# One shared probability tile for both key blocks in a sliding-window attention, and square roots on ScalarE for the last norms

## The chip, the cores and the metric

The kernel runs on one core of a Trainium2 chip. The core has a matrix engine (PE, with its weight loads shown as PEld), a vector engine (DVE), a scalar engine (ACT), a general engine (POOL), and a queue engine (SP) that issues most transfers. Each engine works through its own instructions in a fixed order; semaphores order them between engines. POOL and ACT issue some transfers too; a transfer that adds to what its target holds is issued by POOL.

The metric is the device time of one execution in microseconds, the median of several runs. Before the change it is 973.95 us (three runs, 972.76 to 975.39).

## The reference

The reference is one layer of a hybrid decoder: 1024 rows and 16 meta rows ahead of them, 1024 columns, in float32.

```python
u = rmsnorm(h, g_pre_mix)
q, k, v, xr, yr = split(u @ w_in)          # 512, 128, 128, 512, 512 columns
attn = sliding_window_attention_with_sinks(q, k, v, sinks)   # 8 heads of 64, 2 key heads, window 128
xr = causal_depthwise_conv(xr, conv_w, conv_b)
rec = gelu(yr) * rg_lru(xr, ...)           # gates, then a scan over the rows
h = h + rmsnorm(concat(attn, rec) @ w_out, g_post_mix)
u = rmsnorm(h, g_pre_ffn)
h = h + rmsnorm(square(relu(u @ w_ff1)) @ w_ff2, g_post_ffn)
return h[:, 16:]
```

In attention, rows are padded in front to a multiple of 128. A block of 128 query rows sees the block of keys before it and its own block. With `diff` the query's position less the key's, a key is valid where 0 <= diff < 128. So in the previous block, query row p sees the key columns c > p, and in its own block the columns c <= p: each of the 128 column numbers is valid in exactly one of the two blocks. For the first block of queries the previous block holds only the 16 meta rows; its other columns are invalid. A sink per head enters the maximum and the denominator of the softmax.

## The kernel before

**Precision.** A float32 product is made of reduced-precision ones (fp32r): each operand is split into a high part (a cast on ACT) and a low remainder (a subtraction on DVE; `split`, lines 93 to 100), and `mm3` (lines 121 to 125) adds three matmuls: high by high, high by low, low by high. These three lines are the largest groups of the profile, whatever the stage.

**Stages.** Rows are normed, transposed and projected in four pieces (lines 230 to 352). `fills` (line 570) holds ten more projections, queries, recurrent inputs and gates. Attention (lines 432 to 523) goes over four head pairs `j`, and for each over two halves of four query blocks: `scores(j, half, q)`, then the next projection by `next_fill`, marked as less urgent by 1000 places (`deferred`), then `attend` for the pair-half before. Then come the gates and the scan of the recurrence (`gates`, `decay`, `recur`, `rec_out`), the output projection, its norm, and the two feed-forward products, made by a Strassen-like plan of sums of quarter matrices. The last product has seven plan entries `i` with eight steps `q` each (`steps`, line 1082); the last three steps of the last entry are run row tile by row tile, each followed by `finish_late`.

**What sets the order.** Within a stage the instructions are written in program order, and the framework orders each engine's instructions ahead of time by priority and by when its own simulation has them ready; `behind` pins single instructions behind others, and `lut` pins the order of table functions on ACT. On the chip the order of each engine is fixed. Buffers come from pools by tag; `bufs` (line 55) gives their number: 8 of tag c, 17 of tag b, 2 of tag raw, 2 of tag e, and so on. An instruction that needs a buffer waits until the last user of it is done.

**Scores.** For each of two heads of the pair-half, and two blocks at a time, PE writes scores against both key blocks, 256 columns, to PSUM (lines 447 and 451). One fused DVE instruction adds the mask, takes the minimum with the negated sink, and writes the negated masked scores with their minimum (`tensor_tensor_reduce`, line 467; `mask1` for block 0). ACT takes the exponential of 257 columns (256 and the sink) with its sum (`lut`, line 474). DVE scales by the reciprocal (line 480).

**Values.** `attend` transposes the 256 probability columns of each of four blocks as two 128x128 tiles (line 495), splits them into high and low, and multiplies with the values. Two neighbouring query blocks share a key block, so a key block's values are the stationary operand for 256 columns, except at the ends (128): ten matmuls a head (line 506, in `av`). Halves of the result are added (lines 520 and 521).

**The values themselves** are transposed from `vt` and split by `put_v` (lines 409 to 422); `vm` holds the 16 meta rows, zero below, and `km` their keys.

**The last stage.** `fetch_2` loads the weights of a step; where a sum of two quarters is wanted, either both are loaded and added on DVE, or the second is added by an accumulating POOL transfer (line 1055). `LASTW` (line 1041) names the buffers for the steps of the last entry: (tag, None) means one buffer with an accumulating transfer. `finish_early` norms the row tiles 4 to 7 and adds them to the output in DRAM by an accumulating transfer. `finish_half` prepares the second half of the tiles 0 to 3, `finish_late` ends them: the tiles 0 and 1 as the early ones, the tiles 2 and 3 with rows read back (`h`) and added by DVE, and two plain stores each. The inverse root of a norm is taken by POOL, as a power of -0.5 (`rstd_of`, line 164, and line 1173).

Of the kernel before, what the change touches and what calls it, by code (L numbers as in the profile page):

```python
# [37 lines left out]
def hybrid_layer(  # L38
# [128 lines left out]

    def load_cols(cols, tag="ws"):
        raw = slot("raw", [P, KC, P])
        o = 0  # L170
        for c0, n in cols:
            w, lo = c0
            nc.sync.dma_start(
                raw[:, :, o : o + n],
                w[:, lo : lo + n].rearrange("(k p) c -> p k c", p=P),
            )
            o += n
        hi, lo_ = pair(tag, [P, KC, P])
        split(hi, lo_, raw)
        return hi, lo_  # L180
# [45 lines left out]
    nc.vector.tensor_copy(vm.rearrange("p a b -> p (a b)"), zero[:, :256])  # L226
# [80 lines left out]
    def sink_k(acc, t0, n):  # L307
        o = 0
        if t0 == 0:
            m = slice(0, NMETA)  # L310
            put_k(
                [km[:, 0, m], km[:, 1, m]], [km[:, 2, m], km[:, 3, m]], acc[:, m]
            )
            o = NMETA
# [8 lines left out]
    def new_q():  # L323
# [3 lines left out]
        def sink_q(acc, t0, n):  # L327
            c = slice(t0 - NMETA, t0 - NMETA + n)
            for h in range(2):
                r, o = HALF[h], HALF[1 - h]  # L330
                split_scaled(q[h][r, c], q[h][o, c], acc[r], HD ** -0.5)
# [25 lines left out]
    for c in range(NLRU):  # L357
# [7 lines left out]
    mask = const.tile([P, 256], F32, name="mask")  # L365
    nc.gpsimd.memset(mask, 0.0)
    nc.gpsimd.affine_select(
        out=mask[:, 0:P], in_=mask[:, 0:P], pattern=[[1, P]], compare_op=ALU.is_gt,
        fill=NEG, base=0, channel_multiplier=-1,
    )  # L370
    nc.gpsimd.affine_select(
        out=mask[:, P:256], in_=mask[:, P:256], pattern=[[-1, P]],
        compare_op=ALU.is_ge, fill=NEG, base=0, channel_multiplier=1,
    )
    mask1 = const.tile([P, 256], F32, name="mask1")
    nc.gpsimd.memset(mask1[:, 0:P], NEG)
    nc.gpsimd.memset(mask1[:, 0:NMETA], 0.0)
    nc.gpsimd.affine_select(
        out=mask1[:, 0:NMETA], in_=mask1[:, 0:NMETA], pattern=[[1, NMETA]],
        compare_op=ALU.is_gt, fill=NEG, base=P - NMETA, channel_multiplier=-1,  # L380
    )
    nc.gpsimd.tensor_copy(mask1[:, P:256], mask[:, P:256])
# [30 lines left out]

    pv = bank("o")
    nc.tensor.transpose(pv[:NMETA, :P], vt[:, :NMETA], ident)
    put_v([vm[:NMETA, 0, :], vm[:NMETA, 1, :]], pv[:NMETA, :P])
    for b in range(2):
# [4 lines left out]
        put_v([vk[0][:, 4 * b : 4 * b + 4, :], vk[1][:, 4 * b : 4 * b + 4, :]], pv)  # L422
# [9 lines left out]
    def scores(j, half, q):  # L432
        sn = [slot("c", [P, 4, 257]) for _ in range(2)]
# [3 lines left out]
        for h in range(2):  # L437
            nc.vector.tensor_copy(
                sn[h][:, :, 256], nsink[:, j + 4 * h : j + 4 * h + 1].to_broadcast([P, 4])
            )  # L440
        for bp in range(2):
            for h in range(2):
# [21 lines left out]
                for i in range(2):  # L464
                    b = 4 * half + 2 * bp + i
                    k = 2 * bp + i
                    nc.vector.tensor_tensor_reduce(
                        out=sn[h][:, k, 0:256], in0=sp_[:, i, :],
                        in1=mask1 if b == 0 else mask, scale=-1.0,
                        scalar=nsink[:, j + 4 * h : j + 4 * h + 1],  # L470
                        op0=ALU.add, op1=ALU.min, accum_out=negm[:, h, k : k + 1],
                    )
                    lut(
                        sn[h][:, k, :], sn[h][:, k, :], AF.Exp, scale=-1.0,
                        bias=negm[:, h, k : k + 1], accum_out=den[:, h, k : k + 1],
                    )
        for h in range(2):
            nc.vector.reciprocal(rden[:, h, :], den[:, h, :])
            for k in range(4):
                nc.vector.tensor_scalar(  # L480
                    sn[h][:, k, 0:256], sn[h][:, k, 0:256], rden[:, h, k : k + 1],
                    None, op0=ALU.mult,
                )
        return sn

    def attend(j, half, sn):
        flat = [t_.rearrange("p a b -> p (a b)") for t_ in sn]
        for h in range(2):
            ph, pl = pair("c", [P, 1024])
            for bp in range(2):  # L490
                pt = bank("pt")
                for i in range(2):
                    for s in range(2):
                        o = (2 * i + s) * P
                        nc.tensor.transpose(  # L495
                            pt[:, o : o + P],
                            sn[h][:, 2 * bp + i, s * P : (s + 1) * P], ident,
                        )
                c = slice(512 * bp, 512 * bp + 512)
                split(ph[:, c], pl[:, c], pt)  # L500
            po = bank("o")

            def av(kb, oc, n, pc, first, last):
                v = vm[:, h, :] if kb == 0 else vk[h][:, kb - 1, :]
                for k, p_ in enumerate((ph, pl)):
                    nc.tensor.matmul(  # L506
                        po[:, oc : oc + n], v, p_[:, pc : pc + n],
                        start=first and k == 0, stop=last and k == 1,
                        skip_group_check=True,
                    )  # L510

            kb0 = 4 * half
            av(kb0, 0, P, 0, True, False)
            for i in range(3):
# [767 lines left out]
```

## Time and profile before

| what | value |
|---|---|
| median of three runs | 973.95 us |
| the profiled execution, in all | 972.95 us |
| its span | 971.1 us |
| granted clock of PE | 0.999 |
| busy: PE, DVE, ACT, POOL | 953.7, 674.6, 502.0, 82.4 us |
| transposes of probabilities (line 495) | 128, 128x128 |
| value matmuls (line 506) | 96 of 256 columns, 64 of 128 columns |
| first and last start of the value matmuls | 73.9 and 216.8 us |
| fused mask and minimum (line 467) | 64, 0.48 us each |
| last matmul of PE starts | 963.7 us |

Times in the views are microseconds from the span's start, and ns where marked. PE's matmuls are pipelined: one's busy time overlaps the next one's, so the cost of a matmul in a row is read from start to start, not from its busy time. In a timeline, a line gives start, length, engine, line of the kernel, operation, what is written and read, and in square brackets the engine's idle time before it with what ended it. The chain is the run of work that ended last, followed back from the end.

### The profile page before, as it was taken

What the parts mean: (1) busy time and instruction counts of PE and PEld (TensorE: products, weight loads), DVE (VectorE), ACT (ScalarE), POOL (GpSimd) and SP (SyncE); (2) the same over time, 40 slices, a digit from 0 to 9 for tenths busy, and PEclk for the clock granted to TensorE, in tenths of its full rate; (3) what the DMA queues carried; (4) which work ended last, traced back from release to release, by engine and by line L of the source; (5) the groups of instructions that cost most, each with busy time, mean ns of one, the idle gap of its engine ahead of it and who ended that gap; (6) DMA issues with size and microseconds to landing.
All of it is one profiled execution on the core that took longest, in us unless ns stands there. A gap on an engine that the chain in (4) does not pass through costs nothing.

```text
span 971.1 us, 12490 instructions
## 1 busy us (share of the span) xinstructions
PE 953.7 (98%) x4782; PEld 803.0 (83%) x4782; DVE 674.6 (69%) x997; ACT 502.0 (52%) x809; POOL 82.4 (8%) x109
## 2 busy tenths in 40 slices
PE   6999999999999999999999999999999999999997
PEld 6999999888878887888888878888888888888786
DVE  6679997775976686665645465468557676779694
ACT  6646673567844554343555556555433344445350
POOL 4100000000002100000000000000111000003152
PEclk9999999999999999999999999999999999999999
DMA  9002001012234466576522264323678765548923
GB/s 296 23 1 66 23 23 44 23 48 64 84 119 144 159 207 209 173 251 209 198 87 87 97 206 125 114 87 114 172 176 198 186 224 187 184 163 195 223 80 87
DMA packets 88219, 130.13 MB, mean 134 GB/s; under 512 B 13624, under 2 KB 52552, under 8 KB 88160
## 3 DMA queue, kind: packets, MB, share of 16 engines
q1 hardware_dynamic: 79792, 107.33, 33.4%
q0 software_dynamic: 7792, 20.45, 10.1%
q10 hardware_dynamic: 576, 1.57, 0.4%
q8 instruction: 37, 0.61, 0.2%
q14 instruction: 22, 0.18, 0.1%
HBM read 110.46 MB, written 18.87 MB: 133 GB/s over the span
## 4 chain that ended last, share of the span: by engine, by line
PE 89%; DVE 4%; DMA 3%; issue 2%; ACT 1%; POOL 0%; SPq 0%; POOLq 0%; DVEq 0%; ACTq 0%
PE ps_acc L124 11%; PE ps_acc L123 11%; PE ps_acc L125 11%; PE ps_s L125 6%; PE ps_pt L123 6%; PE ps_s L124 6%; PE ps_pt L125 6%; PE ps_s L123 6%; PE ps_pt L124 6%; PE ps_o L124 5%; PE ps_o L123 5%; PE ps_o L125 5%; PE ps_o L506 2%; PE ps_pt L495 1%; DMA raw<-in_w_ff_dram 1%
## 5 line engine op out<-in xcount | busy, mean ns | idle before, releaser
L95 ACT CAST ws<-raw 128x1024 fp32r<-128x1024 f32 (+1 forms) x69 | 70.7, 1024 | 126.6 <-PE ps_o L124 48.8
L98 DVE TENSOR_TENSOR ws<-raw,ws 128x1024 fp32r<-128x1024 f32 (+1 forms) x70 | 83.5, 1194 | 59.6 <-ACT ws L95 59.5
L123 PE MATMUL ps_acc<-a,ws 128*128 128x256 f32 (+2 forms) x272 | 90.5, 333 | 0.6 <-DVE b L305 0.6
L124 PE MATMUL ps_acc<-a,ws 128*128 128x256 f32 (+2 forms) x272 | 89.8, 330 | 0.0
L125 PE MATMUL ps_acc<-a,ws 128*128 128x256 f32 (+2 forms) x272 | 89.4, 329 | 0.0
L98 DVE TENSOR_TENSOR b<-b,b 128x1024 fp32r<-128x1024 f32 (+2 forms) x48 | 57.6, 1201 | 24.7 <-PE ps_o L124 17.1
L95 ACT CAST ws<-e 128x1024 fp32r<-128x1024 f32 x43 | 45.0, 1046 | 55.3 <-PE ps_o L124 28.1
L95 ACT CAST b<-b 128x1024 fp32r<-128x1024 f32 (+2 forms) x48 | 49.4, 1030 | 42.8 <-DVE b L788 40.0
L98 DVE TENSOR_TENSOR ws<-e,ws 128x1024 fp32r<-128x1024 f32 x43 | 52.6, 1222 | 21.6 <-ACT ws L95 21.6
L123 PEld LDWEIGHTS ps_acc<-a,ws 128*128 128x128 f32 x272 | 51.2, 188 | 4.9 <-DVE b L305 0.8
L125 PEld LDWEIGHTS ps_acc<-a,ws 128*128 128x128 f32 x272 | 51.2, 188 | 4.6
L124 PEld LDWEIGHTS ps_acc<-a,ws 128*128 128x128 f32 x272 | 51.2, 188 | 3.9
L164 POOL TENSOR_TENSOR rs<-ms,half_pow 128x1 f32<-128x1 f32 (+1 forms) x31 | 21.3, 692 | 356.5 <-DVE ms L160 355.1
L123 PE MATMUL ps_acc<-ws,b 128*128 128x512 f32 (+1 forms) x120 | 46.3, 386 | 0.4 <-ACT ws L95 0.4
L124 PE MATMUL ps_acc<-ws,b 128*128 128x512 f32 (+1 forms) x120 | 46.5, 388 | 0.2 <-DVE ws L98 0.2
L125 PE MATMUL ps_acc<-ws,b 128*128 128x512 f32 (+1 forms) x120 | 46.2, 385 | 0.0
L123 PE MATMUL ps_pt<-ws,b 128*128 128x512 f32 x112 | 44.1, 394 | 0.0
L124 PE MATMUL ps_pt<-ws,b 128*128 128x512 f32 x112 | 44.1, 394 | 0.0
L125 PE MATMUL ps_pt<-ws,b 128*128 128x512 f32 x112 | 44.0, 393 | 0.0
L123 PE MATMUL ps_s<-ws,b 128*128 128x512 f32 x110 | 43.4, 395 | 0.0
L124 PE MATMUL ps_s<-ws,b 128*128 128x512 f32 x110 | 43.3, 393 | 0.0
L125 PE MATMUL ps_s<-ws,b 128*128 128x512 f32 x110 | 43.3, 393 | 0.0
(381 smaller groups left out, 2690.1 us busy)
## 6 DMA issues: line engine op xcount, KB each, us to landing
raw<-in_w_ff_dram SPq DMA_DIRECT2D x62, 512.0 KB, 4.0
e<-in_w_ff_dram SPq DMA_DIRECT2D x45, 512.0 KB, 3.6
d<-in_w_ff_dram SPq DMA_DIRECT2D x12, 512.0 KB, 3.8
s_dram<-d POOLq DMA_DIRECT2D x12, 512.0 KB, 3.9
raw<-in_w_in_dram SPq DMA_DIRECT2D x9, 512.0 KB, 3.6
c<-in_x_dram SPq DMA_DIRECT2D x8, 512.0 KB, 8.5
d<-in_x_dram SPq DMA_DIRECT2D x8, 512.0 KB, 4.6
out_dram<-raw SPq DMA_DIRECT2D x8, 512.0 KB, 2.6
```

The costliest lines, as they stand in the source:

```text
L95: nc.scalar.copy(hi, src)
L98: low = nc.vector.tensor_tensor(lo, src, f32(hi), op=ALU.subtract).ins
L123: nc.tensor.matmul(dst, lh, rh, start=start, stop=False, skip_group_check=True)
L124: nc.tensor.matmul(dst, lh, rl, start=False, stop=False, skip_group_check=True)
L125: nc.tensor.matmul(dst, ll, rh, start=False, stop=stop, skip_group_check=True)
L164: nc.gpsimd.tensor_tensor(rs[:n], ms[:n], half_pow[:n], op=ALU.pow)
L495: nc.tensor.transpose(pt[:, o : o + P], sn[h][:, 2 * bp + i, s * P : (s + 1) * P], ident,)
L506: nc.tensor.matmul(po[:, oc : oc + n], v, p_[:, pc : pc + n], start=first and k == 0, stop=last and k == 1, skip_group_check=True,)
```

## The change

One probability tile is kept for both key blocks. Scores are written negated (queries are scaled by -1/8). ACT copies the own block's scores from PSUM, and DVE overwrites them with the previous block's where the mask `above` (column > row) is set: 128 columns a block in place of 256. For query block 0 the columns below 112 are set to a large number where `above` holds, and the meta rows now sit at the end of their block (columns and rows 112 to 127 of `km` and `vm`). The minimum with the sink is a reduction over 129 columns for four blocks at once, the exponential has 129 columns, and one multiplication scales four blocks. These buffers need one c buffer a pair-half instead of two.

In `attend`, each head has four transposes instead of eight. With P the transposed shared tile, and M the part of it that belongs to the own block (selected by POOL from both the high and the low tile), the result is V_previous P + (V_own - V_previous) M. So the values of the previous block multiply the whole tile, and differences of neighbouring blocks (`vd`, made by POOL and split) multiply the selected one: sixteen matmuls of 128 columns a head.

In the last stage, inverse roots are a square root on ACT and a reciprocal on DVE (`root_rstd`); `load_root` loads ACT's table ahead. Eps is added by ACT. Row tile 2 is ended as the tiles 0 and 1 are, with an accumulating store. For tile 3, the product with the gain is made for each part. The first entry of `LASTW` has tag b instead of raw.

```diff
+    eps_col = const.tile([P, 1], F32, name="eps_col")
+    def load_root():
+        nc.gpsimd.memset(eps_col, EPS)
+        root = small.tile([P, 1], F32, name="root", tag="root")
+        lut(root, eps_col, AF.Sqrt)
+    def root_rstd(ssq, bias, n=P):
+        sd = small.tile([P, 1], F32, name="sd", tag="sd")
+        lut(sd[:n], ssq, AF.Sqrt, bias=bias)
+        rs = small.tile([P, 1], F32, name="rs", tag="rs")
+        nc.vector.reciprocal(rs[:n], sd[:n])
+        return rs[:n]
...
-    nc.vector.tensor_copy(vm.rearrange("p a b -> p (a b)"), zero[:, :256])
...
-                split_scaled(q[h][r, c], q[h][o, c], acc[r], HD ** -0.5)
+                split_scaled(q[h][r, c], q[h][o, c], acc[r], -(HD ** -0.5))
...
+    vmt = const.tile([P, P], F32, name="vmt")
+    nc.gpsimd.memset(vmt, 0.0)
+    nc.gpsimd.tensor_copy(vmt[:, P - NMETA :], vt[:, :NMETA])
+    vm_f = const.tile([P, P], F32, name="vm_f")
+    vf, vdf = slot("c", [P, 8, P]), slot("c", [P, 8, P])
+    vd = [slot("c", [P, 8, P], F32R) for _ in range(2)]
...
+    nc.gpsimd.tensor_tensor(vdf[:, 0, :], vf[:, 0, :], vm_f, op=ALU.subtract)
+    nc.gpsimd.tensor_tensor(
+        vdf[:, 1:, :], vf[:, 1:, :], vf[:, : 7, :], op=ALU.subtract
+    )
+    put_v(vd, vdf)
...
-        for bp in range(2):
-            for h in range(2):
+        for h in range(2):
+            for bp in range(2):
...
-                    nc.vector.tensor_tensor_reduce(
-                        out=sn[h][:, k, 0:256], in0=sp_[:, i, :],
-                        in1=mask1 if b == 0 else mask, scale=-1.0,
...
+                s_ = sn[:, h, 2 * bp : 2 * bp + 2, 0:P]
+                nc.scalar.copy(s_, sp_[:, :, P:256])
+                nc.vector.copy_predicated(
+                    s_, above_i.rearrange("p (a b) -> p a b", a=1).to_broadcast([P, 2, P]),
+                    sp_[:, :, 0:P],
+                )
...
+            nc.vector.tensor_reduce(
+                negm[:, h, :], sn[:, h], axis=mybir.AxisListType.X, op=ALU.min
+            )
...
+            nc.vector.tensor_tensor(
+                sn[:, h, :, 0:P], sn[:, h, :, 0:P],
+                rden[:, h, :].to_broadcast([P, 4, P]), op=ALU.mult,
+            )
...
+            for i in range(4):
+                nc.tensor.transpose(pt[:, i * P : (i + 1) * P], sn[:, h, i, 0:P], ident)
+            pt = pt.rearrange("p (a b) -> p a b", a=4)
+            split(ph[:, 0], pl[:, 0], pt)
+            for p_ in (ph, pl):
+                nc.gpsimd.affine_select(
+                    out=p_[:, 1], in_=f32(p_[:, 0]), pattern=[[0, 4], [1, P]],
+                    compare_op=ALU.is_ge, fill=0.0, base=0, channel_multiplier=-1,
                 )
...
+            for s in range(2):
+                for i in range(4):
+                    b = 4 * half + i
+                    v = vd[h][:, b, :] if s else vk[h][:, b - 1, :] if b else vm[:, h, :]
+                    for k, p_ in enumerate((ph, pl)):
+                        nc.tensor.matmul(
+                            po[:, i * P : (i + 1) * P], v, p_[:, s, i, :],
...
     LASTW = [
-        ("raw", None), ("e", "raw"), ("b", None), ("b", None), ("raw", "e"), ("b", None),
+        ("b", None), ("e", "raw"), ("b", None), ("b", None), ("raw", "e"), ("b", None),
...
+        nc.scalar.activation(ssq[0], ssq[0], AF.Identity, bias=eps_col)
+        rs = root_rstd(ssq[1], ssq[0])
...
-        if j > 1:
+        if j > 2:
             h = slot("d", [P, D])
             nc.sync.dma_start(h, out[j * P : (j + 1) * P, :])
-            nc.gpsimd.tensor_scalar(ssq, ssq, EPS, None, op0=ALU.add)
...
-            if j < 2:
+            if j < 3:
...
+            if k == 1:
+                rs = root_rstd(ssq, 0.0)
+            w_low[0] = combine(o[:, c], acc[:, c], gffn_b[:, c], ALU.mult).name
...
-        nc.gpsimd.tensor_tensor(rs, ssq, half_pow, op=ALU.pow)
```

## The prediction

> **What bounds the kernel now.** I read the page first: its busy times, then its chain.
>
> ```profile
> PE 953.7 (98%) x4782; PEld 803.0 (83%) x4782; DVE 674.6 (69%) x997; ACT 502.0 (52%) x809; POOL 82.4 (8%) x109
> ...
> PE 89%; DVE 4%; DMA 3%; issue 2%; ACT 1%; POOL 0%; SPq 0%; POOLq 0%; DVEq 0%; ACTq 0%
> ```
>
> PE is busy for 98% and makes 89% of the chain. A busy PE may still stand in pipelined stretches, so the stage that changes was read next, in windows (columns: length, then busy time of PE, PEld, DVE, ACT, POOL, clock, DMA).
>
> ```profile
> 85.00:100.00 15.00, 15.00 (x117) 14.39 (x116) 14.71 (x41) 12.59 (x32) 0.00 (x0) 1.00 0.12 36
> 130.00:145.00 15.00, 15.00 (x130) 15.00 (x129) 14.76 (x55) 11.55 (x38) 0.00 (x0) 1.00 0.08 23
> ...
> 245.00:275.00 30.00, 29.59 (x128) 23.64 (x128) 30.00 (x28) 24.26 (x31) 0.00 (x0) 1.00 0.19 67
> ```
>
> Attention runs from 52 to 219 us. DVE is nearly full there, POOL idle, and PE is full all the same: projections fill its gaps. The view of PE's waits from 50 to 222 us is empty, and from 50 to 300 us it has one wait, 0.4 us at 271.8. So lighter DVE work buys nothing in this stage; what counts is the time that PE's own instructions take. That is read from starts in PE's timeline, and from runs of one kind in the chain.
>
> ```profile
> 88.11 0.22 PE L447 MATMUL ps_s<-km,b 128*128 128x128 f32 x1
> 88.17 0.28 PE L451 MATMUL ps_s<-km,b 128*128 128x128 f32 x1
> 88.28 0.27 PE L447 MATMUL ps_s<-b,b 128*128 128x128 f32 x1
> 88.39 0.28 PE L451 MATMUL ps_s<-b,b 128*128 128x128 f32 x1
> 88.50 0.33 PE L447 MATMUL ps_s<-b,b 128*128 128x256 f32 x1
> ```
> ```profile
> 116.97 1.00 PE ps_o L506 x9
> 117.97 0.90 PE ps_pt L495 x8
> ```
>
> Four matmuls with 128 columns follow each other: the first start-to-start is 0.06 us, the next three 0.11. Their 0.19 us weight loads start 0.11 us apart too. A 256-column matmul takes 0.12 in a row (73.33 to 73.45). So halving the width of a matmul saves almost nothing once several stand in a row. Nine value matmuls take 1.00 us, eight transposes 0.90.
>
> **Attention on PE.** There are 16 head tiles (4 pairs, 2 halves, 2 heads).
> - Transposes: 8 become 4 a head tile, 64 fewer in all; 64 x 0.11 = -7.0 us.
> - Value matmuls: before 4 of 128 and 6 of 256 columns, 4 x 0.11 + 6 x 0.118 = 1.15 us; afterwards 16 of 128, 16 x 0.11 = 1.76. The difference times 16 is +9.8 us. Its bounds are 0.06 a matmul (15.4 us in all against 18.4, so -3.0) and 0.115 (+11.0). I take 0.11, since the four above stand in a row as the new ones will.
> - Scores, projections and the number of value transposes stay.
>
> PE has +2.8 us more to do, and no idle time before it to put that in.
>
> The Trainium skill (TensorE: Matmul & The Clock Gate, section Back-to-back issue gap) gives 81 ns for a sustained matmul of 128 columns; by it the value matmuls would cost 20.7 us, +2.3, and the whole change would end near 967.7 us. The trace does not agree: 0.11 in a row. The same page's section on LDWEIGHTS, 128 columns at 1.2 GHz or 107 ns, does agree.
>
> **Attention beside PE**, for each of 8 pair-halves. DVE loses 8 fused mask-and-minimum steps of 0.480 + 0.083, 8 scalings of 0.350, 2 subtractions of 0.686 and 2 copies of 0.159: 9.0 us. It gains 4 predicated copies of 256 columns (0.42, like other 256-column reads of PSUM), 2 reductions and 2 multiplications of 512 columns (0.69): 4.5 us. The trace has no predicated copy; its bounds are 0.35 (the scaling) and 0.69. DVE gets some 35 us lighter over the stage. ACT gains 4 copies of 0.373 and loses 2 casts of 0.584 and half the width of 8 exponentials: about even. All this lies beside PE's projections: 0. If the cover went, one head tile's chain (copies 1.5, reduction 0.7, exponentials 2.8, scaling 0.7) would be bare, near 6 us.
>
> POOL gains 4 selects of 128x512. The trace has 128x128 selects of 0.328 and 0.468 us; times four that is 1.3 to 1.9 each, 5 to 8 us in a pair-half of some 20. They stand between the split and the second eight value matmuls, which DVE's subtraction fed directly before. The first eight need no mask and give 0.88 us, and PE has projection matmuls to put between: 0, with the first rival as its upper end. A gain is excluded, as nothing waited here.
>
> **Value preparation and setup.** Three more ACT copies, two halves of `vd` split on ACT and DVE (0.62 and 0.69 each), and one POOL subtraction of 1024 columns (no row; at least the 0.96 of a 128x1024 memset). They lie under the 11 us of projections (52.9 to 58.6, 60.1 to 65.8) ahead of the first value matmul at 73.9: 0, and about +4 if bare. The masks' POOL work at 1 to 3 us, the zeroing of `vm` on DVE and the columns of `km` lie under the first weight load, which lands at 9.5: 0.
>
> **The first step of the last product.** Its weights arrive late.
>
> ```profile
> 907.68 9.19 DMA raw<-in_w_ff_dram
> 916.96 1.05 ACT ws L95
> 918.03 1.24 DVE ws L98
> ```
> ```profile
> 917.25 0.40 PE L125 MATMUL ps_o<-ws,b 128*128 128x512 f32 x1
> 918.05 0.50 PE L123 MATMUL ps_acc<-ws,b 128*128 128x512 f32 x1 [0.40 <-ACT ws L95]
> ...
> 918.86 0.28 PE L123 MATMUL ps_o<-ws,b 128*128 128x256 f32 x1
> 919.31 0.50 PE L124 MATMUL ps_acc<-ws,b 128*128 128x512 f32 x1 [0.18 <-DVE ws L98]
> ```
>
> The gaps cost PE 0.57 + 0.11 + 0.33 + 0.11 = 1.1 us over its usual spacing. POOL issued this accumulating load at 907.68, behind four transfers of its own. With a buffer of tag b, SP's first half can start when the first b load did (884.4, not 893.0), and POOL's half goes ahead of the others: -1.1. Bounds: -1.1, and 0 if POOL's order stays. Late next are the other b loads, each one place back in SP's queue: the last would issue after 906.4, and it is used past 940.
>
> **The end.** The eps additions on POOL (6.0 and 7.2 us, hidden) go, early norms trade POOL's power for ACT and DVE (hidden: PE runs on), and row tile 2 trades SP's load and two stores for one accumulating POOL store. What sets the end is tile 3.
>
> ```profile
> 965.29 0.99 POOL L1173 TENSOR_TENSOR rs<-part,half_pow 128x1 f32<-128x1 f32 x1 [2.87 <-DVE part L1165]
> ```
> ```profile
> 966.31 1.41 DVE L1177 SCALAR_TENSOR_TENSOR a<-a,rs,d 128x512 f32<-128x512 f32 x2 [0.44 <-POOL rs L1173]
> ```
>
> From the accumulator's end (965.14) to DVE's product are 1.17 us. A root on ACT of 128x1 (0.19, like an accumulator read), a reciprocal of 0.17 and two handovers of 0.05 to 0.15 make 0.5 to 0.7: -0.5, with bounds 0 (DVE puts the 0.4 us gain product first) and -0.7. Tile 2's store comes close: sum at 959.79, squares and root until 961.7, product of 1.29, then 0.64 to the issue and 5.1 to landing (as tiles 0 and 1 have it) gives 968.7, against 969.3 for tile 3's last store.
>
> **Sum:** 2.8 - 1.1 - 0.5 = +1.2. The profiled execution has 971.1 us of span and 972.95 in all, 1.0 below the median 973.95. So it would take 974.15, and the median 975.2.
>
> **Rivals.**
> 1. *POOL's masks come late and PE waits* (slower). Each head tile's second mask ends 2.6 to 3.8 us after the split. PE's order is fixed beforehand; where it allows 1 us too little in each pair-half, that is 8 x 1 = +8 and 983. It decides once masks are later than the 0.88 us of plain matmuls plus whatever projections stand between. For it: this row, where a 128x1 addition took 6 to 7 us beside a full DVE, against 0.22 elsewhere (L158).
> ```profile
> L1144 POOL TENSOR_SCALAR late<-late x2: 6041/6641/7241, 931.7 to 939.6; 128x1 f32<-128x1 f32 x2
> ```
> Against it: DVE is lighter in the new attention. The Trainium skill (GPSIMD Engine Reference, section Key points) says that POOL shares its SBUF interfaces with DVE and contends with instructions of two SBUF inputs; this row agrees.
> 2. *The recurrence after attention starts late.* DVE is full from 245 to 275 and PE already waits 0.6 to 0.8 us at 271. Gates need all eight c buffers; `vd` holds two until the last value matmul. If they start 3 us later against PE, those are bare: +3, 978.2. Against it: lighter DVE can pull convolutions and splits ahead.
> 3. *The late edits don't gain.* The (6, 0) gap stays (+1.1), or tile 2's store takes the 7 to 10 us that such stores took between 884 and 912 and ends the kernel (+2 to +3): about 977.
> 4. *Narrow matmuls at 0.06 us* (faster): -3.0 - 7.0 - 1.6 gives 962.4. Against it are the three 0.11 above; for it, lone ones at 0.06, each followed by a lengthened one.
>
> **How the numbers follow.** Forecast 0.45 (its own range 973.6 to 977.0: the 271 us wait gone too, or half of the gains missing), rival 1 0.23, rival 2 0.14, rival 3 0.11, rival 4 0.07. The range 972.5 to 984 leaves out rival 4 and the upper part of rival 1. A measurement of this kernel tells about 0.3%, 2.9 us, from no change. Within it lie nearly all of the forecast (0.43) and some of rival 3 (0.04): same 0.47. Slower is the rest of these, 0.45; faster 0.08.
>
> **What would show it.** Right: 64 transposes and 256 value matmuls at 0.11 us start to start, no waits of PE on POOL, attention ending some 3 us later, no gap near 918, root and reciprocal in 0.7 us at the end. Wrong: waits of PE or ACT on the selected tiles, a longer gap ahead of the output projection's second half, value matmuls closer than 0.1 us, or an accumulating store that lands last.

## The result and the profile after

The changed kernel takes 979.77 us (median of six runs, 979.0 to 980.28) beside 973.36 us of the kernel before (six runs, 972.31 to 975.39). The ratio is 1.0059 with a 95% interval of 1.0046 to 1.0072: slower, by 4.5 to 7.0 us. Its profiled execution takes 980.23 us with a span of 978.5, which is 7.4 us more than the 971.1 of the one before. The sum had forecast 1.2 of these. The page of the kernel after, first its busy times and then its chain:

```profile
PE 957.2 (98%) x4814; PEld 804.9 (82%) x4814; DVE 656.5 (67%) x844; ACT 503.6 (51%) x850; POOL 97.1 (10%) x149
...
PE 88%; DVE 4%; ACT 4%; DMA 3%; issue 1%; SPq 0%; DVEq 0%; ACTq 0%
```

PE still bounds the kernel. ACT's share of the chain went from 1% to 4%. The value matmuls now stand at line 536 and the transposes at 519; in the chain of the kernel after, runs of them read so:

```profile
96.75 0.46 PE ps_pt L519 x4
...
110.32 1.74 PE ps_o L536 x16
```

Sixteen value matmuls of 128 columns take 1.74 us, 0.109 each, and four transposes 0.46. The next view is that of PE's waits in the kernel after, from 50 to 300 us; the kernel before has one wait there, of 0.4 us.

```profile
PE ps_acc L123 <- ACT c L353: 1.1, 1, 1.1
PE ps_pt L123 <- ACT b L95: 0.7, 1, 0.7
PE ps_s L470 <- DVE c L489: 0.6, 1, 0.6
PE ps_pt L124 <- DVE a L98: 0.2, 1, 0.2
```

No wait is on POOL. Two of the four lie where the values are prepared and the first scores are masked (71.3 and 88.6 us), two where the output projection waits for the recurrence (272 to 277 us). The account of the span, from the starts of PE's instructions in the two traces; "extra time" is what PE takes from start to start over its usual spacing (0.11 us, and 0.23 for 512 columns in proportion):

| place | before, us | after, us | difference |
|---|---|---|---|
| value matmuls, start to start | 17.9 (160 of them) | 27.3 (256) | +9.4 |
| transposes of probabilities, without the stall at 88.6 | 12.1 (128) | 5.5 (64) | -6.6 |
| extra time at 50 to 100 us | 0.7 | 3.4 | +2.7 |
| extra time at 250 to 300 us | 0.7 | 1.4 | +0.7 |
| extra time at 375 to 475 and 575 to 600 us | 0.2 | 2.0 | +1.8 |
| extra time at 900 to 950 us | 1.8 | 0.2 | -1.7 |
| from the last matmul's start to the end | 7.3 | 8.0 | +0.7 |

These make +7.0 of the 7.4; the rest lies in differences of 0.3 us and less. The first two rows are the +2.8 of the forecast; the sixth is its -1.1, and larger. The seventh, the end, was in it as -0.5; the other three were put at nothing.

### The profile page after: what moved, and what is told of

Its sections match the earlier page's. It is cut to its first block, busy times and chain, and to the rows that moved or that the text cites. A ratio compares the mean times of both kernels' runs of the same rounds, so it can differ in the third digit from the quotient of the medians.

```text
span 978.5 us, 12504 instructions
## 1 busy us (share of the span) xinstructions
PE 957.2 (98%) x4814; PEld 804.9 (82%) x4814; DVE 656.5 (67%) x844; ACT 503.6 (51%) x850; POOL 97.1 (10%) x149
## 4 chain that ended last, share of the span: by engine, by line
PE 88%; DVE 4%; ACT 4%; DMA 3%; issue 1%; SPq 0%; DVEq 0%; ACTq 0%
PE ps_acc L124 10%; PE ps_acc L123 10%; PE ps_acc L125 10%; PE ps_pt L123 6%; PE ps_pt L125 6%; PE ps_pt L124 6%; PE ps_s L125 6%; PE ps_s L123 6%; PE ps_s L124 6%; PE ps_o L125 5%; PE ps_o L123 5%; PE ps_o L124 5%; PE ps_o L536 3%; ACT c L82 1%; PE ps_s L470 1%; DMA b<-t_dram 1%
## 5 line engine op out<-in xcount | busy, mean ns | idle before, releaser
L123 PE MATMUL ps_o<-ws,b 128*128 128x512 f32 (+1 forms) x108 | 41.5, 384 | 0.0
```

What stands on the lines that cost most here:

```text
L123: nc.tensor.matmul(dst, lh, rh, start=start, stop=False, skip_group_check=True)
```

## The experiments

The theory after the comparison: narrow value matmuls cost more than the saved transposes bring; the differences of values delay the first scores and leave PE without cover; row tile 2's new store holds up the last ones. Each part was then taken alone or undone.

### e1: the attention part alone

The edit leaves the last stage as it was in the kernel before.

```diff
-        ("b", None), ("e", "raw"), ("b", None), ("b", None), ("raw", "e"), ("b", None),
+        ("raw", None), ("e", "raw"), ("b", None), ("b", None), ("raw", "e"), ("b", None),
...
-    load_root()
...
-        if j > 2:
+        if j > 1:
...
```

> The kernel after with its last stage as before: only the attention part, the preparation of values and the setup are changed. The theory puts the loss there: in the two profiles the value matmuls go from 17.9 us for 160 to 27.3 us for 256 (+9.4) and the transposes from 12.1 to 6.3 (-5.9), so PE's work grows by 3.5 us; PE stands 2.7 us more between 50 and 100 us, while the values are prepared and the first scores are late; 0.7 us more is waited for the recurrence at 271 to 277 us; and about 1 us lies in other stages. That gives +7 to +8 against the kernel before, about 981 us. The rival has it that the last stage's edits cost what they were to save, so that the attention part costs no more than the whole change: +5.5 to +6.5, at most 980 us.

Measured: 981.03 us, ratio 1.0063 (1.0046 to 1.0081) to the kernel before, whose median on this chip was 974.05. The medians give +7.0, the ratio +6.1 with bounds of 4.5 to 7.9. So the attention part makes the loss. The two kernels' intervals overlap too far to tell from this run alone whether the last stage brings a little; e2 tells that.

### e2: the last stage alone

```diff
-        ("raw", None), ("e", "raw"), ("b", None), ("b", None), ("raw", "e"), ("b", None),
+        ("b", None), ("e", "raw"), ("b", None), ("b", None), ("raw", "e"), ("b", None),
...
+    load_root()
...
-        if j > 1:
+        if j > 2:
...
```

> The kernel before with the last stage's edits alone: the first buffer of late weights, the root on ScalarE with a reciprocal, and row tile 2 ended by an accumulating store. The theory from the two profiles: the gap at 917 us goes (-1.7), the last norm is shorter (1.17 to 0.57 us, -0.6), but the last stores of row tile 3 land 3.5 us after their issue instead of 2.05 behind row tile 2's accumulating store (+1.4): together about -1, 972.4 us beside 973.4 of the kernel before. The rival: the gap that goes comes back at another step, or the two effects at the end are larger, and the time is 973.4 or more.

Measured: 972.79 us beside 974.05, ratio 0.9985 (0.9976 to 0.9995): -1.3 by the medians, as the theory has it. In its trace PE's extra time at 900 to 950 us is gone (1.8 us before), and from the last matmul's start to the end it takes 7.8 us in place of 7.3. One stall of 0.9 us stands at 467 us, where a split of weights is late; the kernel before has none there, and attention is the same in both. The kernel after has it at 447.6:

```profile
PE ps_s L125 <- DVE ws L98: 0.5, 1, 0.5
```

Its place changes from kernel to kernel (446 to 449 us in e1 and e4, none near there in e6), so the 1.8 us at 375 to 475 and 575 to 600 us aren't put down to any one edit. What causes them was not tried and stays open.

### e4: row tile 2 ended as before

```diff
-        if j > 2:
+        if j > 1:
...
-            if j < 3:
+            if j < 2:
...
-            if k == 1:
+            if k == len(parts) - 1:
                 rs = root_rstd(ssq, 0.0)
...
```

> The kernel after, with row tile 2 ended as before (its rows of the residual loaded back, two plain stores) and all else kept, the root on ScalarE included. The theory: row tile 2's accumulating store, issued at 970.87 us of the profile, keeps the DMA engines busy until 976.28 and delays row tile 3's two stores behind it, which land 2.9 and 3.5 us after their issue against 2.05 before. With it gone the end comes 1.3 to 1.4 us sooner: about 978.4 us beside 979.8. The rival: the stores are slow for another reason, and the second pass over row tile 2 costs VectorE what it did before: 979.8 or more.

Measured: 978.42 us, ratio 1.0039 (1.0025 to 1.0053) where the kernel after has 1.0059: -1.4 by the medians. The two intervals overlap, so the traces have to carry the reading. The timeline of the kernel after at its end, and then that of e4 (start, length, engine; SPq and ACTq are issues of transfers):

```profile
970.87 0.86 POOL L1190 DMA_DIRECT2D out_dram<-a  x1 [3.63 <-issue]
...
972.08 0.20 ACT L82 ACTIVATE sd<-part 128x1 f32<-128x1 f32 x1 [3.73 <-DVE part L1193]
972.08 0.42 DVE L812 TENSOR_TENSOR a<-a,a 128x256 f32<-128x256 f32 x1
972.42 0.15 DVE L179 RECIPROCAL rs<-sd 128x1 f32<-128x1 f32 x1
972.61 1.41 DVE L1204 SCALAR_TENSOR_TENSOR a<-a,rs,d 128x512 f32<-128x512 f32 x2
973.39 0.36 SPq L1207 DMA_DIRECT2D out_dram<-a  x1
974.06 0.35 ACTq L1207 DMA_DIRECT2D out_dram<-a  x1
```

```profile
971.26 0.35 ACTq L1207 DMA_DIRECT2D out_dram<-a  x1
...
973.53 1.41 DVE L1204 SCALAR_TENSOR_TENSOR a<-a,rs,d 128x512 f32<-128x512 f32 x2
974.97 0.35 ACTq L1207 DMA_DIRECT2D out_dram<-a  x1
```

In the kernel after, the last store is issued at 974.06 and the span ends at 978.5, 4.5 us later. In e4 it is issued at 974.97 and the span ends at 978.3, 3.3 us later, as in the kernel before (967.76 and 971.1). The difference is the accumulating store of row tile 2, issued at 970.87: the trace has its pieces landing until 976.28, and the two plain stores of row tile 3 only behind them, at 977.0 and 977.55. From the last matmul's start to the end it takes 7.1 us in e4 and 8.0 in the kernel after. So the theory holds. The root itself did what was forecast: from the accumulator's end at 972.04 to DVE's product at 972.61 are 0.57 us, 1.17 before.

### e5: narrow value matmuls in the kernel before

```diff
             for i in range(3):
-                av(kb0 + 1 + i, i * P, 256, P + 256 * i, False, False)
+                for s in range(2):
+                    av(kb0 + 1 + i, (i + s) * P, P, P + 256 * i + s * P, False, False)
```

> The kernel before with one edit: each value matmul of 256 columns is issued as two of 128, with the same weights and the same additions: 96 matmuls more, no masks, differences or moves. The theory: on TensorE 128 columns take as long as 256 here (0.11 us), so the value matmuls go from 17.9 to 27.3 us as in the kernel after, and nearly all of it is time, less the 0.8 us that PE waits at 271 us for the recurrence anyway: +8 to +9.4, about 982.5 us. The rival: PE has slack between the pieces of attention, other engines set the pace there, and less than half of it shows: +2 to +5, 976 to 979.

Measured: 985.39 us, ratio 1.0107 (1.0080 to 1.0134), which is +7.8 to +13.1 us, somewhat above the theory's 982.5. The rival is out: a narrow matmul costs its whole 0.11 us here. The chain of the profile shows eight of them:

```profile
97.03 0.84 PE ps_o L506 x8
```

From starts, the value matmuls went from 17.9 to 26.8 us (+8.9). Another 1.8 us stands at 375 to 400 us, the kind of stall that e2 has at 467.

### e6: the differences on VectorE

```diff
-    nc.gpsimd.tensor_tensor(vdf[:, 0, :], vf[:, 0, :], vm_f, op=ALU.subtract)
-    nc.gpsimd.tensor_tensor(
+    nc.vector.tensor_tensor(vdf[:, 0, :], vf[:, 0, :], vm_f, op=ALU.subtract)
+    nc.vector.tensor_tensor(
         vdf[:, 1:, :], vf[:, 1:, :], vf[:, : 7, :], op=ALU.subtract
```

> The kernel after with the subtraction of neighbouring value blocks on VectorE and not on POOL, in the same buffers. The theory: POOL's subtraction of 128x896 takes 2.64 us and stretches a VectorE pass beside it to 1.81 us (0.41 alone), and it stands ahead of POOL's copies for the first scores; with it gone the stalls at 84.9 (0.24 over the usual spacing) and 88.6 us (0.75) go, the one at 71.3 us (1.2, behind ScalarE's order) stays: -1, about 978.8 us. The rival: the first scores wait for buffers of tag c, of which the value blocks and their differences hold six of eight at that time, and for VectorE's splits of them; then the three stalls stay and the time is 979.8 or more.

Measured: 978.80 us, ratio 1.0039 (1.0027 to 1.0051): -1.0 by the medians, as the theory says. The interval overlaps that of the kernel after, so here too the traces decide. First POOL and DVE in the timeline of the kernel after, then DVE in that of e6:

```profile
73.66 2.64 POOL L441 TENSOR_TENSOR c<-c 128x896 f32<-128x896 f32 x1 [13.50 <-ACT c L438]
76.25 2.54 POOL L461 COPY c<-nsink 128x4 f32<-128x4 f32 x4
```
```profile
74.77 2.15 DVE L98 TENSOR_TENSOR b<-c,b 128x256 fp32r<-128x256 f32 x2
```
```profile
75.33 1.09 DVE L441 TENSOR_TENSOR c<-c 128x896 f32<-128x896 f32 x1
76.35 0.75 DVE L98 TENSOR_TENSOR b<-c,b 128x256 fp32r<-128x256 f32 x2
```

The subtraction takes 1.09 us on DVE and 2.64 on POOL, and the two DVE passes that ran beside it take 0.75 us in place of 2.15. PE's waits at 50 to 100 us in e6 are one line:

```profile
PE ps_acc L123 <- ACT c L353: 1.1, 1, 1.1
```

The stalls at 84.9 and 88.6 us are gone, PE's extra time at 75 to 100 us falls from 1.4 to 0.35 us; the stall at 71.3 us stays.

### e3: two selects, values as plain blocks

```diff
-            split(ph[:, 0], pl[:, 0], pt)
+            split(ph[:, :, 0], pl[:, :, 0], pt)
             for p_ in (ph, pl):
                 nc.gpsimd.affine_select(
-                    out=p_[:, 1], in_=f32(p_[:, 0]), pattern=[[0, 4], [1, P]],
+                    out=p_[:, :, 1], in_=f32(p_[:, :, 0]), pattern=[[0, 4], [1, P]],
                     compare_op=ALU.is_ge, fill=0.0, base=0, channel_multiplier=-1,
                 )
+                nc.gpsimd.affine_select(
+                    out=p_[:, :, 0], in_=f32(p_[:, :, 0]), pattern=[[0, 4], [-1, P]],
+                    compare_op=ALU.is_gt, fill=0.0, base=0, channel_multiplier=1,
+                )
...
+            for i in range(5):
+                b = 4 * half + i
+                v = vk[h][:, b - 1, :] if b else vm[:, h, :]
+                c = slice(max(0, 256 * i - P), min(1024, 256 * i + P))
...
-    vf, vdf = slot("c", [P, 8, P]), slot("c", [P, 8, P])
-    vd = [slot("c", [P, 8, P], F32R) for _ in range(2)]
```

> The kernel after, but POOL selects both parts of each tile of probabilities (the own block's in the second half, the rest in place in the first), so that values enter as plain blocks in the 256-column matmuls of the kernel before, and no differences of values are made. The 64 saved transposes stay. The theory says that the 96 extra narrow matmuls and the differences of values are the cost: -9.4 us of value matmuls and -2.7 us of stalls at 50 to 100 us, so 979.8 - 12.1 = 967.7 us (966 to 969.5), below the kernel before by 4 to 7 us. A rival puts the stalls at 50 to 100 us on the shared tile's scores (copy, predicated copy, one reduction for four blocks) and not on the differences: then they stay and the time is about 970.4. Another rival: POOL's doubled selects (four for each head pair, 0.65 us each in the profile of the kernel after, 2.6 us for each head tile pair) come late and PE waits for them: 972 us or more.

Measured: 973.51 us, ratio 0.9989 (0.9978 to 0.9999). That is 6 us less than the kernel after and not the 12 of the theory. Both parts of the theory show in the trace: without stalls, value matmuls and transposes take 23.1 us in place of 32.8 (-9.7), and the extra time at 50 to 100 us is 0.7 in place of 3.4 (-2.7), so the first of the two rivals is out. The late weights at 447 us are absent and the stall at 586 is smaller (-1.1). But 4.1 us came back at 150 to 158 us, 0.8 at the recurrence, and 2.7 at 216, 379 and 758 us. PE's waits of e3 from 40 to 300 us:

```profile
PE ps_pt L123 <- ACT b L95: 1.8, 1, 1.8
PE ps_o L534 <- POOL c L519: 1.3, 1, 1.3
PE ps_acc L123 <- ACT d L353: 1.1, 1, 1.1
```

A wait on POOL's second select (line 519) is in front at 150 us, so the second rival looked right, there alone. The next runs went after it.

### e7: two buffers held

```diff
+    hold = [slot("c", [P, 8, P]) for _ in range(2)]
+    for t_ in hold:
+        nc.gpsimd.memset(t_[:, 0, 0:1], 0.0)
...
+    for t_ in hold:
+        held = small.tile([P, 1], F32, name="held", tag="held")
+        nc.gpsimd.tensor_copy(held, t_[:, 0, 0:1])
```

> The kernel with two selects for each tile of probabilities (e3), but two of the eight buffers of tag c are held from the preparation of values to the end of attention, as the differences hold them in the kernel after; no work is added but two copies of one column. Theory of the buffers: with six left the scores of one head pair can't run ahead of the products of the one before, and part of the stalls of the kernel after at 50 to 100 us (2.7 us) comes back: +1 to +3, 974.5 to 976.5. Theory of the work: the copies, subtraction and splits are what delays the first scores, and the held buffers cost nothing there: 973.5, PE's extra time at 50 to 100 us as in e3 (0.7 us).

Measured: 973.59 us, as e3, and PE has no wait at 50 to 100 us. The two buffers that the differences hold through attention cost nothing. That leaves the work of preparing them, ahead of the first scores, or the four buffers that this takes for a moment; these two were not tried apart.

### e8, e9, e10: whose is the stall at 150 us?

e8 takes e3 with row tile 2 ended as in e4, and masks the low parts of the last head pair on DVE. e9 leaves POOL's second select out of e3, and with it a part of the computation, to price that select alone. e10 is e8 with the condition `p_ is pl` alone, so that DVE masks all low parts. The two masks `own` and `rest` are made at setup. The core of e8:

```diff
+                if p_ is pl and j == 3:
+                    for s, m in ((1, own), (0, rest)):
+                        m = m.rearrange("p (a b) -> p a b", a=1).to_broadcast([P, 4, P])
+                        nc.vector.tensor_tensor(
+                            p_[:, :, s], f32(p_[:, :, 0]), m, op=ALU.mult
+                        )
+                    continue
```

> e3 with two edits: row tile 2 ended as before (e4), and for the last head pair the low parts are masked by multiplications on VectorE, the high parts by POOL's selects; the zero padded meta tile takes a buffer of tag c. The theory: the stalls of e3 at 150.6 and 153.1 us (together 2.8 us more than the usual spacing, 4.4 us in that stretch) are POOL's selects, of which single ones take 2.18 and 1.52 us instead of 0.63 beside VectorE's passes; with half of them on VectorE the stretch costs 1 to 2 us, and the end is 1.3 us shorter: 973.5 - 1.3 - 3 = 969 us (968 to 970.5). The rival: the recurrence behind attention sets the time there (PE waits 2.2 us for it at 263 us in e3) and takes the gain back; then only the end is shorter, 972 us.

> e3 without the second select: the shared tile enters whole where only the part of the block before is due, so the own part's probabilities are counted for both blocks. That leaves out part of the computation, to price POOL's second select by itself; matmuls, splits and buffers stay those of e3. The theory: in e3 PE stands 4.4 us more than in the kernel after at 150 to 155 us because single selects take 2.18 and 1.52 us beside VectorE's passes (0.63 else) and follow one another on POOL; with half of them gone the stretch costs at most 1 us: 973.5 - 3.5 = 970 us (969 to 971), if what follows takes none of it back. The rival: the scheduled order around there (value matmuls ahead of a projection, ScalarE's copy behind them) holds PE by itself, and the selects are no more than its longest part: 972.5 to 973.5.

> e8 with the low parts of all head pairs, not of the last alone, masked by multiplications on VectorE, so that POOL makes two selects for each head tile instead of four (e8 has the stalls at 150.8 and 153.5 us as before, which lie in the second head pair, not in the last). The theory: the stretch at 150 to 155 us, 4.5 us over the usual spacing in e8, falls to 1 or 2 and the kernel comes to 969 to 970 us beside 972.2 of e8. The rival: VectorE, with 32 passes of 0.65 us more (some 20 us between 70 and 215 us), falls behind and takes the gain away, there or at the recurrence behind it (PE waits 1.8 us at 263 in e8): 972 to 974 us.

Measured: e8 972.17 us, ratio 0.9975 (0.9963 to 0.9987); e9 974.14, 0.9996 (0.9983 to 1.0010); e10 974.07, 0.9996 (0.9984 to 1.0008). The gain of e8 is that of the end: from the last matmul's start it takes 7.05 us in place of 8.0. The stretch at 150 to 155 us stayed, since it belongs to the second head pair and not to the last, which the edit touches. In e9, with half of the selects, PE's extra time from 150 to 175 us is still 4.1 us, and in e10 it is 6.3. So the theory of the selects falls, and both rivals hold. DVE in the timeline of e9 shows the cause:

```profile
148.62 3.09 DVE L553 SCALAR_TENSOR_TENSOR d<-d,prm,d 128x1039 f32<-128x1039 f32 x2
151.74 0.69 DVE L98 TENSOR_TENSOR c<-ps_pt,c 128x512 fp32r<-128x512 f32 x1
152.35 1.29 DVE L553 SCALAR_TENSOR_TENSOR d<-d,prm,d 128x1037 f32<-128x1037 f32 x1
```

ACT had the cast of the probabilities done at 149.9, but their low part (line 98) comes at 151.74 behind two passes of a convolution (line 553). The select then runs beside the next pass:

```profile
152.50 1.63 POOL L515 TENSOR_SCALAR_AFFINE_SELECT c<-c 128x512 fp32r<-128x512 f32 x1 [0.62 <-DVE c L98]
```

### e11: the convolution's passes behind

The edit collects a convolution's DVE instructions, emits them two rounds of `attend` later, and pins them behind the last low part of that round.

```diff
-            conv(c, xr, "b" if c == 3 else "d")
+            late_conv.append(lambda c=c, xr=xr: conv(c, xr, "b" if c == 3 else "d"))
...
+            lag.append(late_conv[:])
+            del late_conv[:]
+            if len(lag) > 2:
+                for run in lag.pop(0):
+                    behind(low_mark[0], *run())
```

> e8 with the four VectorE passes of each later convolution (1.13, 1.28, 1.28 and 1.3 us) ordered behind the low parts of the head pair that they run among at 144 to 152 us; nothing else is changed. e9 showed the stretch at 150 to 155 us as long with half of POOL's selects. The theory: what holds PE there is VectorE's order, in which these passes stand between the casts and the low parts of the probabilities (and stretch the select beside them), and half of what is lost is TensorE's clock, granted at 0.5 for about 2.5 us behind the waits: with the passes behind, the 4.5 us over the usual spacing fall to 1 or less and the kernel comes to 968 to 970 us beside 972.2 of e8. The rival: the passes are needed by the gates and the recurrence soon after; then the wait goes to the start of the gates or to 263 us (1.8 us in e8) and the time stays at 971.5 to 973.

Measured: 968.68 us, ratio 0.9927 (0.9908 to 0.9946). This beats the kernel before by 5 to 9 us, and by the two ratios the kernel after by 1.3%. Not all of it is the shared tile's: the last stage's edits alone brought 1.3 us in e2, and e11 also ends row tile 2 as e4 does. The stretch from 150 to 155 us in windows (length, then busy time of PE, PEld, DVE, ACT, POOL, clock, DMA), of e8 and of e11:

```profile
150.00:155.00 5.00, 2.44 (x18) 1.85 (x16) 3.15 (x4) 1.73 (x4) 4.86 (x9) 0.94 0.00 0
155.00:157.00 2.00, 2.00 (x10) 2.00 (x11) 0.13 (x1) 0.10 (x1) 0.15 (x1) 0.50 0.00 0
```
```profile
150.00:155.00 5.00, 5.00 (x45) 5.00 (x44) 2.07 (x3) 1.91 (x4) 2.72 (x6) 1.00 0.01 3
```

PE goes from 18 matmuls to 45 in the same 5 us, and its clock stays whole. The wait didn't move to the recurrence: PE's extra time at 250 to 275 us is 1.7 us, 1.8 in e8.

### e12: the same order in the kernel before

```diff
                 split(ph[:, c], pl[:, c], pt)
+            low_mark[0] = mark[0]
             po = bank("o")
...
+                    behind(low_mark[0], *run())
```

> The kernel before with the order of e11 alone: the passes of each later convolution behind the low parts of the head pair that they would run among. It tells whether e11's gain (968.7 us) is the order's by itself. The theory: the kernel before has no stall at 100 to 225 us that the order could take away (PE busy 25.0 of 25 us in each stretch, at most 0.35 us over the usual spacing), so the order is worth nothing without the shared tile: 973.5 to 975, no difference from the kernel before. The rival: VectorE's order also moves the start of the recurrence, for which PE waits 0.8 us at 271 us in the kernel before, and the splits of weights; then it is 1 to 5 us faster, and that much of e11's gain is not the shared tile's.

Measured: 979.96 us, ratio 1.0062 (1.0044 to 1.0080): slower, which neither side expected. So this order brings nothing by itself; it pays with the shared tile. Whether another order would pay in the kernel before was not tried. PE's waits of e12 from 100 to 225 us, where the kernel before has none:

```profile
PE ps_s L447 <- DVE negm L467: 1.3, 1, 1.3
PE ps_o L509 <- DVE c L98: 1.0, 1, 1.0
PE ps_acc L123 <- ACT d L339: 0.8, 1, 0.8
PE ps_o L509 <- ACT c L95: 0.2, 1, 0.2
```

The passes have moved to 175 to 200 us, where DVE has most to do already: it is busy for 24.7 of 25 us in e12 and for 20.2 in the kernel before, and PE's extra time there is 3.4 us. DVE's timeline of e12 shows a pass between the minima that PE waits for, and a split of weights ahead of the low parts. In e11 the passes stand at much the same time (176 to 183 us) and DVE is as full, 24.6 of the 25 us, but PE is busy for 24.9 of them.

```profile
190.60 0.50 DVE L467 CUSTOM_DVE_ANT_0 c<-ps_s,mask,nsink 128x256 f32<-128x256 f32 x1
191.01 0.10 DVE L467 DVE_READ_ACCUMULATOR2_ANT negm<- 128x1 f32 x1
191.01 1.31 DVE L538 SCALAR_TENSOR_TENSOR d<-d,prm,d 128x1037 f32<-128x1037 f32 x1
192.22 0.49 DVE L467 CUSTOM_DVE_ANT_0 c<-ps_s,mask,nsink 128x256 f32<-128x256 f32 x1
...
193.02 1.24 DVE L98 TENSOR_TENSOR ws<-raw,ws 128x1024 fp32r<-128x1024 f32 x1
194.16 1.30 DVE L98 TENSOR_TENSOR c<-ps_pt,c 128x512 fp32r<-128x512 f32 x2
```

## Where the prediction was right and where it was wrong, point by point

The time lies in the range given, 972.5 to 984.0, but it is not that of the forecast. The result is slower by 0.6%, twice the bound of 0.3% within which the forecast lay. The span grew by 7.4 us and not by 1.2. That the range holds it is in part luck: the upper part of the range was there for POOL's masks, which cost nothing, and what came in their place stood in the sum at nothing or as a gain.

- **Attention on PE, +2.8: right.** The transposes brought 6.6 us (7.0 forecast), the value matmuls cost 9.4 (9.8). e5 confirms the larger term by itself, 7.8 to 13.1 us. The fourth rival, narrow matmuls at 0.06 us, is out: sixteen in a row take 0.109 each. The Trainium skill (TensorE: Matmul & The Clock Gate, section Back-to-back issue gap) would have them at 81 ns; this trace does not agree.
- **Attention beside PE, 0: right, with a wrong size.** No wait came from lighter or heavier work between 95 and 225 us. POOL's select was forecast at 1.3 to 1.9 us and takes 0.636 in the median, so the first rival had no ground here. DVE did not get 35 us lighter: its busy time fell by 18.1 over the whole kernel, with the preparation of values and the last norms in it. The working added up busy times of instructions that overlap; the kernel before starts its fused steps 0.405 us apart, not 0.56.
- **Value preparation and setup, 0: the step that failed.** It was put under the projections ahead of the first value matmul at 73.9 us, with "about +4 if bare". The cover that it named, projections until 65.8 us, ends before the longer part of the chain can begin: the second half of the values is transposed only at 71.16 us (at 72.87 in the kernel before), and one subtraction makes the differences of seven of the eight blocks, at 73.66. Behind it come the splits of the differences, and behind these, in ACT's order, the first copies of scores (line 488):

```profile
72.99 0.59 ACT L438 COPY c<-ps_pt 128x512 f32<-128x512 f32 x1
...
76.33 1.15 ACT L95 CAST c<-c 128x512 fp32r<-128x512 f32 x2 [2.01 <-POOL c L441]
77.38 0.64 ACT L488 COPY c<-ps_s 128x256 f32<-128x256 f32 x2
```

The bracket is ACT's wait for POOL's subtraction. In e3, without differences, the first such copy of scores starts at 53.47 us. The first exponential of the kernel after starts at 84.4 us (61.8 in e3), and the first value matmul at 92.8. In the kernel before, PE has 18 instructions of attention to fill the time at 72.9 to 74.9 us, while ACT is behind with a cast of weights and a projection's copy; in the kernel after it has two transposes there, and waits 1.1 us from 71.5. In all, this stretch cost 2.7 us. e6 shows that 1.0 of it is POOL's subtraction; e3, which has no differences, shows the rest going with them; e7 shows that it is not the two buffers that they keep. Whether the rest comes from the work and its order or from the four buffers taken for a moment stays open.

- **First step of the last product, -1.1: right, and more.** The gaps went whole: 1.7 us by the extra time at 900 to 950 us.
- **The end, -0.5: half wrong.** The root took 0.57 us as said. The step that failed is row tile 2's store: it was only asked whether it lands ahead of row tile 3's (968.7 against 969.3), and not what it does to them. DVE's product for it started at 969.04 behind tile 3's first addition, and 0.55 us of issue came on top; it landed at 976.28, 5.4 us after its issue. That is ahead of tile 3's stores, but the last of these took 3.5 us to land in place of 2.05. The end became 0.7 us longer; e4 takes 1.4 back by the medians, 1.0 in its trace.
- **The recurrence, second rival: there, but small.** +0.7 us and not 3. e7 speaks against its reason, the two buffers that `vd` holds.
- **Not in the prediction:** 1.8 us of late weights and sums at 375 to 475 and 575 to 600 us, which come and go between kernels.

So the case that happened is parts of the second and third rivals together with a cover that was missing; the chance of 0.45 for slower was for its larger half POOL's masks, which cost nothing.

e11 shows what the shared tile can bring, by a step that the prediction did not look at: a select is cheap enough to be made twice, so that the values can keep 256 columns. Without the narrow matmuls PE is fast enough for DVE's order to become the bound at 150 us, which hid 4 us of e3's gain.

## What to carry to other kernels

Where a matmul of 128 columns takes as long in a row as one of 256 (0.11 and 0.12 us here), count instructions, not columns: 96 more matmuls, each half as wide, cost 9.4 us, more than the 6.6 that 64 saved transposes brought. A preparation that stands ahead of the first use must be costed as a chain, from the last input that it waits for to the first instruction that needs it, with each engine's queue behind it, even if all of it is short; and a saving on the bounding engine should be followed to the next order of another engine that it runs into, which can be moved. Here an accumulating store near the end delayed the plain stores issued behind it (3.5 us to landing, 2.05 without it), so its landing has to be counted against them too.

## What the runs showed of the hardware

POOL and DVE slow each other far more than their rows elsewhere tell. POOL's select of 128x512 has a median of 0.636 us and took up to 2.18 in e8 and 3.99 in e10, beside DVE passes with two inputs:

```profile
149.18 3.99 POOL L531 TENSOR_SCALAR_AFFINE_SELECT c<-c 128x512 fp32r<-128x512 f32 x1 [0.69 <-DVE c L98]
```

The reverse is in the kernel after, where of two equal DVE passes the first took 1.81 us beside POOL's subtraction and the second 0.41. The Trainium skill (GPSIMD Engine Reference, section Key points) names this sharing of the interfaces to SBUF; the trace agrees and gives its size.

Short waits of PE can halve its clock. In e7, the matmul that starts at 261.4 us is followed by the next one 2.2 us later, with PE idle for 1.8 of them, and then the clock is granted at 0.50 from 265 to 268 us (windows of e7; the clock is the third number from the end):

```profile
261.00:263.00 2.00, 0.80 (x4) 0.31 (x2) 1.75 (x2) 1.99 (x4) 0.00 (x0) 1.00 0.00 0
263.00:265.00 2.00, 1.36 (x5) 1.10 (x6) 1.91 (x3) 2.00 (x4) 0.00 (x0) 0.94 0.00 0
265.00:268.00 3.00, 3.00 (x9) 2.31 (x8) 3.00 (x3) 0.06 (x1) 0.00 (x0) 0.50 0.53 178
```

The same wait, of 1.8 us after the matmul at 263.0 in e3, left the clock at 1.00, while two waits of 1.1 to 1.4 us at 150 to 155 us were followed by 0.50 for about 3 us in e3 and e8. The Trainium skill (TensorE: Matmul & The Clock Gate, Part 1: The HAM clock gate) lets the clock fall after an idle window of some 3.4 us whose phase runs freely; a free phase fits that equal waits differ, but here 1.8 us of idle time were enough. Of the 4.5 us that e8 lost from 150 to 158 us, this was an estimated 1.5 (3 us at half the clock).
